# Layer 0 of a hybrid decoder: 111 two-input elementwise instructions issued on VectorE instead of GpSimd

## The chip, the core and the metric

The program runs on one core of one Trainium2 chip. A core has five engines that run side by side, each through its own queue in order: PE (TensorE, matrix products), DVE (VectorE), ACT (ScalarE), POOL (GpSimd) and SP (which here only issues DMAs). PE writes its products to PSUM; DVE, ACT and POOL work on tiles in SBUF, and DVE and ACT also read PSUM. The metric is device microseconds of one execution. Of the kernel before, three runs took 1946.46, 1949.92 and 1953.49 us; the median, 1949.92 us, is the time to compare with.

## The reference

One inference step of a trunk of two layers, 1024 wide, over a prompt of 1024 rows and 8 samples of 4 rows. All is float32. Layer 0 is cut down here to what the change touches; layer 1 (RWKV-7) is not touched.

```
xn = rmsnorm(h, norm_w[0])
u, z_a, q, f, i, z_b = split(xn @ even_w_in)              # 24 blocks of 128 columns
# S5: 32 groups of 16 channels, 64 complex states each
bu = einsum(u, bb);  h_t = ab * h_{t-1} + bu_t            # complex, as a scan
y  = Re(einsum(h, c)) + d * u
y  = gelu(y);  out_a = y * sigmoid(y @ glu_w + glu_b) * silu(z_a)
# HGRN2: 4 heads, a 128x128 state each
log_f = log_sigmoid(f);  k = sigmoid(-f);  q = silu(q)
S_t = diag(f_t) S_{t-1} + k_t v_t^T;  o_t = S_t^T q_t     # in chunks
out_b = o * rsqrt(mean(o*o) + eps) * hgrn_norm_w * silu(z_b)
h = h + concat(out_a, out_b) @ even_w_out
# layer 1: h = h + rwkv7(rmsnorm(h, norm_w[1]));  y = rmsnorm(h, final_norm_w)
```

## The kernel before

The 1056 rows of tokens lie along the free axis, in two halves of 512 and 544 columns (`HALF`; the second holds the samples). A feature tile is 128 partitions by 512 or 544 columns.

A dense product (`dense2`, line 805) is done in three passes: weights and inputs are each split into a high part (ACT copies it rounded, line 70) and a low part (the rest, by a subtraction, line 72), and PE sums high·high, high·low and low·high. `split` does this; with `lo_pool` the subtraction goes to POOL, otherwise to DVE. Weights come by DMA in pieces of 128x512, are split on ACT and DVE, and two buffers of each part stand ready (`wh`, `wl`).

Layer 0 first normalizes the inputs (`normed`: a product on DVE, line 153, then a split, whose subtraction goes to POOL for every second of the 8 feature tiles), for the second half, the first half, and the second half again when it is reloaded. Then three generators run interleaved in `layer0`: `dense` (`proj_in`, the 20 blocks per half that aren't u), `s5s` (8 calls of `s5_part`, four channel groups each) and `heads` (8 calls of `hgrn_head`: four heads for each half). After `proj_in` follow `glu` and `proj_out` of the first half, with `norm1` for layer 1, whose sum of squares is added up over the 8 tiles (line 843); then the same for the second half beside the start of layer 1.

`s5_part` makes tables (two products, line 410, and their sum, line 412), rotations (lines 444, 445 and 446), brings them onto the scan's inputs (lines 460 to 465), scans (line 467) and rotates back (lines 470 to 477). `hgrn_head` takes the gates through a running sum (lines 570 to 573, 599, 600), makes keys and queries for sub-chunks of 32 rows (lines 611 and 614), and lets PE transpose and multiply them. POOL did one of each pair of products in S5, and five instructions of each head (six in the second half, with line 680).

All instructions go through a scheduler: the code is emitted as the generators yield, and the scheduler, by a model of the engines' costs, sets the order of each engine's queue for the whole program. An edit that moves work from one engine to another can therefore shift the order of instructions anywhere, in layer 1 too, with the same instructions in it.

Lines 64 and 66 are copies out of PSUM on ACT and DVE (`evac`); line 404 transposes S5's C tables on PE through one of three PSUM buffers, which a copy has to clear (`cst`, `csw`); lines 626 to 691 are HGRN2's matmuls, 417 to 493 S5's.

Of the kernel before, what the change touches and what calls it, by code (L numbers as in the profile page):

```python
# [14 lines left out]
ALU = mybir.AluOpType  # L15
# [4 lines left out]
NB, NS = 8, 4  # L20
# [16 lines left out]
class Builder:  # L37
# [111 lines left out]
    def normed(self, hf, k, x):  # L149
        n = HALF[hf][1]  # L150
        with self.tc.high_priority():
            y = self.evt("xn")
            self.nc.vector.scalar_tensor_tensor(out=y[:, :n], in0=x[:, :n], scalar=self.nw0[:, k:k + 1],
                                                in1=self.rbc[hf][:, :n], op0=ALU.mult, op1=ALU.mult)
            h, l = self.pair(n)
            self.split(h[:, :n], l[:, :n], y[:, :n], lo_pool=k % 2 == 1)
        return h, l
# [225 lines left out]
    def s5_part(self, sp, m, e):  # L383

        nc, I = self.nc, self.I
        V, G = nc.vector, nc.gpsimd
# [21 lines left out]
        for out, n, pa, pb, sa, sb in ((X, 8, self.xr, self.xi, bst, bsw), (Gt, 9, self.gr, self.gi, cst, csw)):  # L408
            for w, o, p, x in ((V, t1, pa, sa), (G, t2, pb, sb)):
                w.tensor_tensor(out=o[:, :, :n], in0=p[:, gs].unsqueeze(3).broadcast_to([128, 4, n, 16]),  # L410
                                in1=x[:].unsqueeze(2).broadcast_to([128, 4, n, 16]), op=ALU.mult)
            V.tensor_tensor(out=out, in0=t1[:, :, :n], in1=t2[:, :, :n], op=ALU.add)
# [30 lines left out]
        for out, (p, q), (r, s), op in ((cosn, (ir, jr), (ii, ji), ALU.subtract), (sinn, (ii, jr), (ir, ji), ALU.add)):  # L443
            V.tensor_tensor(out=v4(a1), in0=B(p, 0), in1=B(q, 1), op=ALU.mult)
            G.tensor_tensor(out=v4(a2), in0=B(r, 0), in1=B(s, 1), op=ALU.mult)
            V.tensor_tensor(out=out, in0=a1, in1=a2, op=op)
# [17 lines left out]
        f2 = lambda t: t[:].rearrange("p g c -> p (g c)")  # L464
        G.tensor_tensor(out=r1, in0=r1, in1=r2, op=ALU.add)
        Ht = T("Ht", 4, 128)
        V.tensor_tensor_scan(out=f2(Ht), data0=f2(dec), data1=f2(r1), initial=0.0, op0=ALU.mult, op1=ALU.add)

        m1, m2, ms = T("r1", 4, 128), T("r2", 4, 128), T("tb", 4, 128)
        G.tensor_tensor(out=m2, in0=Ht, in1=sinn, op=ALU.mult)  # L470
        V.tensor_tensor(out=m1, in0=Ht, in1=cosn, op=ALU.mult)
# [79 lines left out]
    def hgrn_head(self, sp, hf, h):  # L551
# [20 lines left out]
        V.tensor_tensor_scan(out=b, data0=self.rs[:, :n], data1=lf, initial=0.0, op0=ALU.mult, op1=ALU.add)  # L572
        G.tensor_tensor(out=f, in0=lf, in1=f, op=ALU.subtract)

# [24 lines left out]
        V.tensor_tensor(out=v33(b), in0=v33(b), in1=rr.unsqueeze(2).broadcast_to([128, nr, 32]), op=ALU.subtract)  # L599
        G.tensor_tensor(out=f, in0=f, in1=b, op=ALU.subtract)  # L600
        A.activation(b, b, AF.Exp)
# [7 lines left out]
        for i in (1, 2, 3):  # L609
            kr[i] = T(f"hk{i}", 4, i + 1, 32)  # L610
            (G if i == 3 else V).tensor_tensor(out=kr[i], in0=v4(kl)[:, :, 0:i + 1], in1=offs[i].unsqueeze(3).broadcast_to([128, 4, i + 1, 32]),
                            op=ALU.mult)
        qi = T("hqi", 4, 4, 32)
        G.tensor_tensor(out=qi, in0=v4(q), in1=wq.unsqueeze(3).broadcast_to([128, 4, 4, 32]), op=ALU.mult)

# [53 lines left out]
        if hf:  # L669
            self.dma(O["p_hgrn"][0, 0, h], self.SH[h])  # L670
            ps = PS(32)
            nc.tensor.matmul(ps, vt[:32, 4], self.atts[:32], start=True, stop=False)
            for s in range(NB):
                cs = slice(512 + NS * s, 512 + NS * s + NS)
                nc.tensor.matmul(ps[:, NS * s:NS * s + NS], S0[:, s], q[:, cs], start=False, stop=s == NB - 1)
            self.evac(o[:, 512:544], ps, 32)
            vm = T("hvm", NB, 128)
            V.tensor_tensor(out=vm[:32], in0=vt[:32, 4].unsqueeze(1).broadcast_to([32, NB, 128]),
                            in1=self.bm[:32].unsqueeze(2).broadcast_to([32, NB, 128]), op=ALU.mult)
            G.tensor_tensor(out=S0, in0=S0, in1=pS.unsqueeze(2).broadcast_to([128, NB, 128]), op=ALU.mult)  # L680
            for c in range(2):
                ps = PS(4, 128)
                nc.tensor.matmul(ps, kt[:32, 4], vm[:32, 4 * c:4 * c + 4], start=True, stop=True)
                V.tensor_tensor(out=S0[:, 4 * c:4 * c + 4], in0=S0[:, 4 * c:4 * c + 4], in1=ps, op=ALU.add)
            self.dma(O["s_hgrn"][0, :, h].rearrange("b k v -> k b v"), S0)
# [8 lines left out]
        V.scalar_tensor_tensor(out=o, in0=o, scalar=self.hw, in1=rst, op0=ALU.mult, op1=ALU.mult)  # L694
        G.tensor_tensor(out=o, in0=o, in1=z, op=ALU.mult)
        self.dma(self.cat_d[h][:, c0:c0 + n], o)
# [124 lines left out]
    def norm1(self, hf, temp):  # L821
# [13 lines left out]
        for k, x in enumerate(self.xn):  # L835
# [4 lines left out]
            if k == 0:  # L840
                V.tensor_copy(acc[:, :n], sq[:, :n])
            else:
                G.tensor_tensor(out=acc[:, :n], in0=acc[:, :n], in1=sq[:, :n], op=ALU.add)
        for p0, q in cuts:
# [1164 lines left out]
```

## Time and profile before

| | |
|---|---|
| median of three runs | 1949.92 us (1946.46 to 1953.49) |
| the profiled execution | 1946.68 us, of which the span 1945.0 us |
| PE busy | 1736.1 us, 89% |
| DVE busy | 1256.1 us, 65% |
| ACT busy | 979.8 us, 50% |
| POOL busy | 507.5 us, 26% |
| granted TensorE clock, mean | 0.903 |

The profile is that of one execution. Busy is time in which an instruction of the engine runs, and an engine that is held up inside an instruction counts as busy. PE's matmuls overlap, so its busy time is more than what it would need. The granted clock is a share of full speed (2.4 GHz); PE runs at either that or 1.2 GHz, and a mean between tells how much of a stretch went at each. Layer 0 takes about the first 645 us, then the two layers overlap to about 770 us.

### The profile page before, as it was taken

The numbers are of one execution on the slowest core, as the hardware profiler recorded it, in microseconds if no ns is written. First come the engines' busy times: TensorE is split into PE (matmuls) and PEld (weight loads), VectorE is DVE, ScalarE is ACT, GpSimd is POOL, SyncE is SP. The second block draws the span as 40 slices with busy tenths as digits, with TensorE's granted clock in tenths as the row PEclk, the third lists the DMA queues.
The fourth block names the chain that finished last, engine by engine and source line by source line (L and its number), as shares of the span: only waits on it lengthen the run. The fifth ranks groups of instructions, "written<-read, shape, count | busy, mean of one in ns | idle before, by whom it ended". The sixth has DMA issues, their size and how long they took to land. (4 is left out here: it accounts for less than half of the span.)

```text
span 1945.0 us, 39798 instructions
## 1 busy us (share of the span) xinstructions
PE 1736.1 (89%) x15060; PEld 1437.8 (74%) x15060; DVE 1256.1 (65%) x2700; ACT 979.8 (50%) x1887; POOL 507.5 (26%) x567
## 2 busy tenths in 40 slices
PE   6989889889979689998579999999899999999977
PEld 5767768788868577576447787888788888778776
DVE  5887778655554953689585852478979454655543
ACT  6345656354553434753345756565547434534464
POOL 2413535323221500001042410133322112331231
PEclk9989989887889899898779997999799899998799
DMA  9545444433544446699928424469795666544453
GB/s 242 150 128 153 112 116 134 121 112 107 154 148 152 128 150 199 199 243 263 247 66 219 140 88 129 130 168 276 191 235 160 164 160 166 151 130 128 121 151 112
DMA packets 555013, 308.40 MB, mean 159 GB/s; under 512 B 284884, under 2 KB 489044, under 8 KB 554821
## 3 DMA queue, kind: packets, MB, share of 16 engines
q1 hardware_dynamic: 554820, 305.86, 57.3%
q8 instruction: 119, 1.95, 0.4%
q14 instruction: 74, 0.60, 0.1%
HBM read 199.76 MB, written 104.81 MB: 157 GB/s over the span
## 5 line engine op out<-in xcount | busy, mean ns | idle before, releaser
L805 PE MATMUL dps<-xh,wh 128*128 128x272 f32 (+3 forms) x1696 | 589.5, 353 | 59.4 <-ACT wh L70 25.0
L805 PE MATMUL dps<-xl,wh 128*128 128x272 f32 (+3 forms) x1696 | 585.3, 347 | 7.8 <-DVE xl L72 6.1
L805 PE MATMUL dps<-xh,wl 128*128 128x272 f32 (+3 forms) x1696 | 581.9, 345 | 5.1 <-DVE wl L72 4.9
L805 PEld LDWEIGHTS dps<-xh,wh 128*128 128x128 f32 x1696 | 335.2, 200 | 110.6 <-ACT wh L70 29.9
L805 PEld LDWEIGHTS dps<-xh,wl 128*128 128x128 f32 x1696 | 338.6, 200 | 48.6 <-DVE wl L72 11.2
L805 PEld LDWEIGHTS dps<-xl,wh 128*128 128x128 f32 x1696 | 338.6, 200 | 47.7 <-DVE xl L72 8.2
L70 ACT ACTIVATE wh<-ws 128x512 fp32r<-128x512 f32 (+1 forms) x336 | 198.8, 620 | 331.8 <-PE dps L805 181.7
L72 DVE TENSOR_TENSOR wl<-ws,wh 128x512 fp32r<-128x512 f32 (+1 forms) x321 | 238.2, 756 | 139.3 <-ACT wh L70 125.5
L1514 PE MATMUL m<-ZR,BK 64*128 64x128 f32 x512 | 68.3, 311 | 10.4 <-DMA ZR<-zr 10.4
L1514 PEld LDWEIGHTS m<-ZR,BK 64*128 64x128 f32 x512 | 56.9, 206 | 19.6 <-DMA ZR<-zr 10.5
L70 ACT ACTIVATE xh<-mm 128x256 fp32r<-128x256 f32 (+1 forms) x112 | 52.9, 483 | 34.0 <-DVE mm L944 15.0
L805 PE MATMUL dps<-gh,wh 128*128 128x272 f32 (+1 forms) x176 | 56.3, 321 | 11.3 <-ACT wh L70 4.3
L72 POOL TENSOR_TENSOR xl<-mm,xh 128x256 fp32r<-128x256 f32 (+1 forms) x40 | 33.1, 828 | 111.6 <-ACT xh L70 89.0
L805 PE MATMUL dps<-gh,wl 128*128 128x272 f32 (+1 forms) x176 | 55.4, 316 | 7.3 <-DVE wl L72 7.3
L805 PE MATMUL dps<-gl,wh 128*128 128x272 f32 (+1 forms) x176 | 55.8, 317 | 5.6 <-DVE gl L72 5.6
L1411 DVE TENSOR_TENSOR sT<-sX,sN 128x31 f32<-128x31 f32 (+15 forms) x124 | 50.3, 405 | 5.2 <-DMA sN<-nd 2.8
L1417 DVE TENSOR_TENSOR sX<-sX,sT 128x31 f32<-128x31 f32 (+15 forms) x124 | 50.8, 410 | 2.3
L72 POOL TENSOR_TENSOR e<-ek,e 128x512 fp32r<-128x512 f32 (+1 forms) x16 | 22.0, 1376 | 114.5 <-ACT e L70 87.9
L72 DVE TENSOR_TENSOR xl<-mm,xh 128x512 fp32r<-128x512 f32 (+2 forms) x72 | 42.6, 599 | 12.7 <-PE t L1104 7.3
L64 ACT ACTIVATE ev<-dps 128x272 f32<-128x272 f32 (+1 forms) x65 | 29.4, 452 | 41.9 <-PE dps L805 36.4
L66 DVE COPY ev<-dps 128x272 f32<-128x272 f32 (+1 forms) x43 | 22.4, 523 | 42.9 <-PE dps L805 36.3
L805 PEld LDWEIGHTS dps<-gh,wh 128*128 128x128 f32 x176 | 36.0, 205 | 16.3 <-ACT ev L723 4.8
(651 smaller groups left out, 3676.4 us busy)
## 6 DMA issues: line engine op xcount, KB each, us to landing
ws<-in_rw_w_rkvz SPq DMA_DIRECT2D x128, 256.0 KB
ws<-in_even_w_in SPq DMA_DIRECT2D x96, 256.0 KB
ws<-in_rw_w_o SPq DMA_DIRECT2D x48, 256.0 KB
ws<-in_even_w_out SPq DMA_DIRECT2D x32, 256.0 KB
BK<-bk SPq DMA_DIRECT2D x32, 256.0 KB
ZR<-zr SPq DMA_DIRECT2D x32, 256.0 KB
pr<-ev SPq DMA_DIRECT2D x20, 272.0 KB
pr<-ev SPq DMA_DIRECT2D x20, 256.0 KB
```

Source lines behind the costliest of these rows:

```text
L64: return self.nc.scalar.activation(out, in_, AF.Copy)
L66: return self.nc.vector.tensor_copy(out, in_)
L70: self.nc.scalar.activation(hi, x, AF.Copy)
L72: e.tensor_tensor(out=lo, in0=x, in1=hi.bitcast(F32), op=ALU.subtract)
L805: mm = lambda c0, n, i, u, k, v: self.nc.tensor.matmul(ps[c0], u[:, k, :], v[:, c0:c0 + n], start=i == 0, stop=i == len(terms) - 1)
L1411: E.tensor_tensor(out=w, in0=X[:, s0:s0 + m, j:j + 1].broadcast_to([128, m, n]), in1=N[:, j, j + 1:32].unsqueeze(1).broadcast_to([128, m, ...
L1417: E.tensor_tensor(out=X[:, s0:s0 + m, j + 1:32], in0=X[:, s0:s0 + m, j + 1:32], in1=w, op=ALU.subtract)
L1514: nc.tensor.matmul(f2(pm[h][:, q]), f2(BK[hr, q]), f2(ZR[hr, q]), start=True, stop=True)
```

## The change

Eleven places of layer 0 issue their two-input instruction on DVE (`V`) where it stood on POOL (`G`). In numbers of instructions: 16 of line 410 and 16 of 445, 8 each of 465, 470, 573, 600, 611 (the key of sub-chunk 3), 614 and 695, 4 of 680, the 7 sums of line 843 for the first half, and 12 subtractions of `normed`. That is 111; POOL's queue is 111 rows shorter, and DVE's longer by as many. The operands, sizes and results are the same.

```diff
@@ normed
-            self.split(h[:, :n], l[:, :n], y[:, :n], lo_pool=k % 2 == 1)
+            self.split(h[:, :n], l[:, :n], y[:, :n])
@@ s5_part: tables, rotations, the scan's input, the rotation back
-            for w, o, p, x in ((V, t1, pa, sa), (G, t2, pb, sb)):
+            for w, o, p, x in ((V, t1, pa, sa), (V, t2, pb, sb)):
-            G.tensor_tensor(out=v4(a2), in0=B(r, 0), in1=B(s, 1), op=ALU.mult)
+            V.tensor_tensor(out=v4(a2), in0=B(r, 0), in1=B(s, 1), op=ALU.mult)
-        G.tensor_tensor(out=r1, in0=r1, in1=r2, op=ALU.add)
+        V.tensor_tensor(out=r1, in0=r1, in1=r2, op=ALU.add)
-        G.tensor_tensor(out=m2, in0=Ht, in1=sinn, op=ALU.mult)
+        V.tensor_tensor(out=m2, in0=Ht, in1=sinn, op=ALU.mult)
@@ hgrn_head: gates, keys, queries, the samples' state, the output's gate
-        G.tensor_tensor(out=f, in0=lf, in1=f, op=ALU.subtract)
+        V.tensor_tensor(out=f, in0=lf, in1=f, op=ALU.subtract)
-        G.tensor_tensor(out=f, in0=f, in1=b, op=ALU.subtract)
+        V.tensor_tensor(out=f, in0=f, in1=b, op=ALU.subtract)
-            (G if i == 3 else V).tensor_tensor(out=kr[i], in0=v4(kl)[:, :, 0:i + 1], in1=offs[i].unsqueeze(3).broadcast_to([128, 4, i + 1, 32]),
+            V.tensor_tensor(out=kr[i], in0=v4(kl)[:, :, 0:i + 1], in1=offs[i].unsqueeze(3).broadcast_to([128, 4, i + 1, 32]),
-        G.tensor_tensor(out=qi, in0=v4(q), in1=wq.unsqueeze(3).broadcast_to([128, 4, 4, 32]), op=ALU.mult)
+        V.tensor_tensor(out=qi, in0=v4(q), in1=wq.unsqueeze(3).broadcast_to([128, 4, 4, 32]), op=ALU.mult)
-            G.tensor_tensor(out=S0, in0=S0, in1=pS.unsqueeze(2).broadcast_to([128, NB, 128]), op=ALU.mult)
+            V.tensor_tensor(out=S0, in0=S0, in1=pS.unsqueeze(2).broadcast_to([128, NB, 128]), op=ALU.mult)
-        G.tensor_tensor(out=o, in0=o, in1=z, op=ALU.mult)
+        V.tensor_tensor(out=o, in0=o, in1=z, op=ALU.mult)
@@ norm1
-                G.tensor_tensor(out=acc[:, :n], in0=acc[:, :n], in1=sq[:, :n], op=ALU.add)
+                (G if hf else V).tensor_tensor(out=acc[:, :n], in0=acc[:, :n], in1=sq[:, :n], op=ALU.add)
```

The scheduler's order moves with it. DVE's queue of the kernel before, at one S5 part's rotations (`cosn` and `sinn` from the products `ta` and `tb`; `tb` is POOL's):

```order
L444 TENSOR_TENSOR ta<-ir,jr 128x512
L72 TENSOR_TENSOR wl<-ws,wh 128x512
L446 TENSOR_TENSOR cosn<-ta,tb 128x512
L72 TENSOR_TENSOR wl<-ws,wh 128x512
L444 TENSOR_TENSOR ta<-ii,jr 128x512
L446 TENSOR_TENSOR sinn<-ta,tb 128x512
L410 TENSOR_TENSOR ta<-xr,bst 128x4x128
```

DVE's queue of the changed kernel, at a part's rotations beside the gates of a head (`hl`, `hf`, `hb`, `hex`) and the second normalization of the reloaded tiles (`xn`, `xl`):

```order
L573 TENSOR_TENSOR hf<-hl,hf 128x512
L72 TENSOR_TENSOR xl<-xn,xh 128x544
L432 TENSOR_TENSOR KK<-KK,dd 16x4x16
L153 SCALAR_TENSOR_TENSOR xn<-x,nw_208,rbc_235 128x544
L446 TENSOR_TENSOR cosn<-ta,tb 128x512
L577 COPY hrr<-hb 128x16
L589 TENSOR_TENSOR hex<-hb 128x4
L72 TENSOR_TENSOR xl<-xn,xh 128x544
L594 MEMSET hrr 128x1
L430 TENSOR_TENSOR dd<-ident,dT 16x64
L444 TENSOR_TENSOR ta<-ii,jr 128x512
L445 TENSOR_TENSOR tb<-ir,ji 128x512
```

Lines 445 and 573 now stand in DVE's own queue between its other work, and every subtraction of `xl` does.

PE's queue of the kernel before where `proj_in` ends (272 columns) and `glu` of the first half begins (`gh`, `gl`, 512 columns); the last head is done by then:

```order
L805 MATMUL dps<-xh,wh 128x272
L805 MATMUL dps<-xl,wh 128x272
L805 MATMUL dps<-xh,wl 128x272
L805 MATMUL dps<-gh,wh 128x512
L805 MATMUL dps<-gl,wh 128x512
L805 MATMUL dps<-gh,wl 128x512
```

The same place in PE's queue of the changed kernel:

```order
L805 MATMUL dps<-xl,wh 128x272
L805 MATMUL dps<-xh,wl 128x272
L805 MATMUL dps<-gh,wh 128x512
L805 MATMUL dps<-gl,wh 128x512
L805 MATMUL dps<-gh,wl 128x512
L626 MATMUL xh<-ident,hk_5403 128x128 x4
L630 MATMUL xh<-ident,hke 32x128
L640 MATMUL xh<-hq,hf 32x32
```

The transposes and products of the last head come after the end of `proj_in` instead of before it. S5's and HGRN2's matmuls between stand later among the dense ones too, by some 50 to 120 places on average.

DVE's queue of the changed kernel during `proj_out` of the first half, where `norm1` adds up its squares (line 843) and `glu` of the second half fetches its inputs (`y`, lines 711 and 713):

```order
L757 TENSOR_TENSOR h_5998<-h_5998,dps 128x512
L72 TENSOR_TENSOR wl<-ws,wh 128x512 x2
L841 COPY n<-n 128x512
L843 TENSOR_TENSOR n<-n 128x512
L757 TENSOR_TENSOR h_6037<-h_6037,dps 128x512
L72 TENSOR_TENSOR wl<-ws,wh 128x512
L711 COPY y<-yl 128x8x64
```

Line 843 was not in this queue before, and the copies of line 711 stood ahead of the first line 757.

## Rows read from the trace of the kernel before

**Rows 1.** The page's head: span, and busy time of each engine.

```profile
span 1945.0 us, 39798 instructions
PE 1736.1 (89%) x15060; PEld 1437.8 (74%) x15060; DVE 1256.1 (65%) x2700; ACT 979.8 (50%) x1887; POOL 507.5 (26%) x567
```

**Rows 2.** Busy time by stretch: us, then PE, PEld, DVE, ACT, POOL, clock, DMA, GB/s.

```profile
200.00:350.00 150.00, 126.95 (x747) 107.26 (x746) 119.11 (x209) 89.08 (x133) 70.86 (x75) 0.91 0.44 122
350.00:560.00 210.00, 193.84 (x1251) 173.56 (x1250) 113.78 (x224) 98.68 (x155) 59.80 (x48) 0.85 0.41 121
1000.00:1945.00 945.00, 883.10 (x10082) 741.51 (x10080) 578.67 (x1282) 496.73 (x1083) 237.60 (x266) 0.92 0.59 157
```

**Rows 3.** What PE waited for from 75 to 645 us: us, times, longest.

```profile
PE xs L404 <- DVE cst L66: 8.1, 1, 8.1
PE dps L805 <- ACT ev L181: 7.3, 7, 1.9
PE dps L805 <- ACT wh L70: 6.6, 1, 6.6
PE xh L626 <- POOL hk L611: 5.1, 3, 3.1
PE xs L458 <- DVE KK L66: 4.7, 2, 4.1
PE dps L805 <- DVE xl L72: 2.3, 1, 2.3
```

**Rows 4.** Line views, one tile Ht on both engines, and two others: ns min/median/max.

```profile
L470 POOL TENSOR_TENSOR r<-Ht,sinn x8: 1266/1616/1802, 190.4 to 477.6; 128x512 f32<-128x512 f32 x8
L471 DVE TENSOR_TENSOR r<-Ht,cosn x8: 672/691/1415, 190.4 to 480.5; 128x512 f32<-128x512 f32 x8
L72 DVE TENSOR_TENSOR xl<-xn,xh x16: 679/712/1855, 25.4 to 1076.8; 128x544 fp32r<-128x544 f32 x8, 128x512 fp32r<-128x512 f32 x8
L678 DVE TENSOR_TENSOR hvm<-hvt,bm x4: 1206/2010/2334, 363.6 to 525.6; 32x1024 f32<-32x1024 f32 x4
```

**Rows 5.** Timeline of DVE and POOL at one rotation: start, us, instruction.

```profile
265.10 0.77 DVE L444 TENSOR_TENSOR ta<-ir,jr 128x512 f32<-128x512 f32 x1
...
265.29 1.50 POOL L445 TENSOR_TENSOR tb<-ii,ji 128x512 f32<-128x512 f32 x1
...
268.02 1.45 POOL L445 TENSOR_TENSOR tb<-ir,ji 128x512 f32<-128x512 f32 x1 [1.23 <-DVE cosn L446]
...
268.47 1.55 DVE L444 TENSOR_TENSOR ta<-ii,jr 128x512 f32<-128x512 f32 x1
```

**Rows 6.** Timeline of DVE: the first and last of 67 stretched rows to 720 us.

```profile
26.22 1.68 DVE L153 SCALAR_TENSOR_TENSOR xn<-x,nw,rbc 128x544 f32<-128x544 f32 x1
...
519.85 1.48 DVE L711 COPY y<-yl 128x512 f32<-128x512 f32 x1
```

**Rows 7.** Waits: DVE's for POOL, 0 to 645 us; last, POOL's at line 680.

```profile
DVE hS L684 <- POOL hS L680: 5.4, 3, 1.8
...
DVE X L412 <- POOL tb L410: 4.6, 2, 3.6
DVE G L412 <- POOL tb L410: 3.8, 3, 1.3
...
POOL hS L680 <- PE xh L675: 27.2, 3, 17.1
```

**Rows 8.** Timeline before PE's longest wait, that for line 404.

```profile
285.42 1.27 POOL L470 TENSOR_TENSOR r<-Ht,sinn 128x512 f32<-128x512 f32 x1 [2.05 <-DVE Ht L467]
285.49 1.28 DVE L590 COPY hex<-hrr 128x4 f32<-128x4 f32 x1
...
290.50 0.36 PE L404 MATMUL xs<-ident,cl 64*128 64x64 f32 x1 [8.13 <-DVE cst L66]
```

**Rows 9.** Granted clock after two of PE's waits: stretches as in rows 2.

```profile
306.00:313.00 7.00, 6.94 (x43) 5.68 (x42) 7.00 (x11) 2.44 (x5) 5.95 (x10) 0.76 0.76 258
...
409.00:413.00 4.00, 4.00 (x21) 4.00 (x22) 4.00 (x19) 1.94 (x3) 0.01 (x1) 0.57 0.46 151
```

## The prediction

> **What bounds the kernel now.** I began with the page's head [rows 1]: PE is busy for 89% of the span, DVE for 65%, POOL for 26%. POOL is no bound by its share; the question is who waits for it, and where. So the second view is busy time by stretch [rows 2], over the part in which most of the moved instructions lie, 79 of the 111. PE has little room there: 127 of 150 us from 200 to 350, 194 of 210 from 350 to 560. Yet it isn't at its best: its clock is granted at 0.91 and 0.85 of full speed. DVE is the second busiest, and from 200 to 350 us nearly full, 119 of 150 us. The third view is what PE waited for [rows 3]. The dense products wait for little; most of the waits are those of S5's and HGRN2's small matmuls, for a DVE copy (8.1 and 4.7 us), for POOL's key `hk` (5.1) and for a split (2.3). These four make 20 us and all end on DVE or POOL. Two more, 7.3 and 6.6 us, end on ACT. A wait costs more than itself: after those near 305 and 409 us the clock stood at 0.76 and 0.57 for 7 and 4 us [rows 9].
>
> So the bound is PE, with short waits in which DVE's queue, in order, has not come to the instruction that PE needs. The last view is why DVE is late: one rotation [rows 5]. The first product on line 444 began 0.19 us before POOL's on line 445 and took 0.77 us. The other, of the same size, began 0.45 us after POOL's next, took 1.55 us, and ended 0.55 us after POOL did. DVE did not work through POOL's instruction; it was held inside its own until POOL ended. Line by line this recurs: line 471 has a median of 691 ns and a longest of 1415, line 72's `xl` 712 and 1855 [rows 4].
>
> **The change part by part.**
>
> *What DVE gets.* 111 instructions. At full width each costs what DVE's twin does undisturbed: 0.69 us at 512 columns (line 471), 0.71 at 544, and 1.21 at 1024 (line 678's shortest) [rows 4]. 107 x 0.70 + 4 x 1.21 = 80 us, of which 30 (43 instructions) lie from 200 to 350 us.
>
> *What DVE loses in stretching.* For every DVE row of the timeline up to 720 us I took its length less the shortest of its line and size. It adds to 89 us. 67 rows, the first and last in [rows 6], are longer by over 0.1 us and lie beside POOL instructions that the change removes more than beside those it leaves: 60 us together, 28 of them from 200 to 350 us. Another 18 us lie beside instructions that stay on POOL and remain. The bounds: 60 if POOL was the cause of each, 0 if POOL only stood beside it. I take 60, since in [rows 5] the end of DVE's instruction follows POOL's end.
>
> *What DVE loses in waiting for POOL.* The sums of lines 684 and 412 waited for POOL's half of a pair, 5.4 + 4.6 + 3.8 = 14 us [rows 7], 1 of them from 200 to 350 us. Now both halves come in one queue.
>
> Together: +80 - 60 - 14 = +6 us over all, and +30 - 28 - 1 = +1 from 200 to 350 us. DVE's queue advances as it did, although 80 us of work came to it.
>
> *What the chains get.* The two-input product took POOL 1.6 us and takes DVE 0.69 [rows 4], so the chains of S5 and HGRN2 shorten by 0.9 us at each of several steps. In PE's longest wait [rows 8], the copy `cst` came 8.1 us late; in these 8 us DVE was held three times by POOL (line 590, a copy of 4 columns, took 1.28 us beside line 470), some 3 us in all by the same reckoning, but now lines 465, 470 and 600 would take 2 us in that queue. This wait shrinks by only 1 us if the order stays, and goes where the order gives it room.
>
> *What the new order gives.* The scheduler puts the small matmuls later among the dense ones, and the last head after `proj_in`'s end. PE's work is the same, and the dense products don't need these results, so PE asks later for what DVE makes at the same pace as before. A hundred places at 150/747 = 0.20 or 210/1251 = 0.17 us a matmul [rows 2] are 17 to 20 us of room, more than any of the four waits. Of the 20 us I therefore take 14 as gone. Bounds: all 20 go, or none, because new ones open elsewhere; I stay nearer to the upper end, as the room exceeds each wait. The clock adds to that: 7 us at 0.76 and 4 us at 0.57 lost 7 x 0.24 + 4 x 0.43 = 3.4 us [rows 9]; I take 3. The 14 us that end on ACT stay: no work leaves ACT.
>
> *What may cost.* The added instructions wait for nearly nothing new: their inputs come from DVE's line before. Two do. Line 680 waits for PE, as it overwrites what line 675 reads; POOL waited there up to 17 us [rows 7]. On DVE the next splits and copies would be queued behind it, and PE waits for those. But in three of the four heads it now stands behind a copy of line 675's result, for which DVE waits anyway. I take 0 to 7 us: nothing in three cases, and in the fourth (27.2 - 17.1)/2 = 5 us, the mean of the two shorter of POOL's waits, and some 2 for what it delays. Line 843 waits for ACT's square, with the next block's `wl` and sum behind it (line 757). It waits for ACT to finish one instruction of a block of 24 matmuls; I take 0, at most 0.7 us x 7 = 5. The last head's DVE work, some 17 instructions' worth at 0.7 us or 12 us, moves into `glu` and `proj_out`, and line 711 after it; there DVE has room, so 0.
>
> *Layer 1.* Its instructions are the same, in an order that differs from 1000 us on. PE is busy for 883 of 945 us there [rows 2], so 62 us are open to chance; a tenth of it, 6 us either way, is my estimate for another order.
>
> Sum: 14 + 3 = 17 us gained, less some 5 for small new waits, half of the 12 that lines 680 and 843 could cost at most: 12 us. The profiled execution took 1946.7 us, 1945.0 of it the span; it comes to 1935. The median of the runs is 3.2 us above that execution, so I forecast 1938 us.
>
> The Trainium skill, "Perfetto Trace Analysis", section "Optimizing Scalar/DVE Operations", speaks against the direction of the move: a saturated DVE may be relieved by giving work to ScalarE or even GpSimd, though it adds that GpSimd shares a port with DVE and that moving between those two might not help. By its first half DVE from 200 to 350 us would go from 119 to 149 of 150 us and the change would lose; by its second half the 28 us come back. The first half is the rival below.
>
> The Trainium skill, "SBUF — State Buffer", section "Who interferes with whom", says that a DVE instruction with two SBUF inputs and a GpSimd instruction that reads SBUF exclude one another for their whole length. The trace agrees, with 1.55 us for 0.77 in [rows 5]. By it the moved instructions can be held in turn by what stays on POOL; that would give back part of the 60 us, an estimate of a quarter, as a quarter of POOL's time in layer 0 stays.
>
> **The rivals.**
>
> *DVE becomes the bound (slower).* If the stretched time isn't POOL's doing, or returns beside what stays there, DVE's queue from 200 to 350 us holds up to 149 us in 150. It then can't take the waits for ACT that it has there, and each `wl` and `xl` comes late for the dense products. Half of the 30 us would land on PE: 1950 + 15 = 1965. It decides from the point where less than about 15 of the 28 us come back. For it: 79% busy already. Against it: [rows 5], and line 590 in [rows 8].
>
> *Nothing to be seen.* The four waits go, and as many open elsewhere: the copies and splits that PE waits for still stand in one DVE queue, now with 111 more rows in front. 1946 to 1950; I put it at 1948. For it: the wait for line 404 shrinks by only 1 us in its own place. Against it: the later asking.
>
> *The order of layer 1 costs more than layer 0 gains.* The whole program was ordered anew. With 6 us more there, and 5 of layer 0's gain left, 1951; a bad place behind a weight's split could make it 1958.
>
> *More than forecast.* All 20 us go, and ACT's 6.6 us with its clock phase: 1950 - 20 - 7 - 5 = 1918.
>
> **How the numbers follow.** Chances: the forecast, between 1928 and 1944, 0.52; more than that 0.10; nothing to be seen 0.20; DVE the bound 0.10; layer 1's order 0.08. The range must leave out no more than two in ten: from 1920, near the best case, to 1958, which holds layer 1's order and leaves out most of DVE as the bound. A measurement of this kernel can tell about 0.3%, 6 us, from no change: faster is below 1944. That is the first two cases, 0.62; the same 0.22 (the third, and a little of the last); slower 0.16.
>
> **What would show it.** Right: DVE's busy time up to 645 us within some 20 us of before, with line 444 near 0.69 us on average, line 72's `wl` too, and no wait of DVE for POOL on lines 412 and 684; PE's waits for `cst`, `hk` and `KK` together below 10 us; the end of `proj_out` of the first half earlier by about 12 us. Wrong: DVE from 200 to 350 us at over 140 of 150 us, with PE waiting for `wl` or `xl`; or layer 0 ending earlier and the span from 1000 us on longer by as much. If line 444 stays near 1 us without POOL beside it, the step on stretching fails, and with it the forecast.

## The result, and the profile of the changed kernel

The changed kernel takes 1926.08 us (median of 4 runs, 1921.69 to 1933.61), beside 1951.70 us (4 runs) for the kernel before: a ratio of 0.9872, 95% interval 0.9829 to 0.9916. The forecast was 1938 us, between 1920 and 1958. The profiled execution took 1924.02 us.

The page's head, which answers to [rows 1], and then what DVE waited for from 75 to 590 us on lines 684, 843 and 680 (us, times, longest; compare [rows 7]):

```profile
span 1922.3 us, 39712 instructions
...
PE 1741.3 (91%) x15060; PEld 1442.8 (75%) x15060; DVE 1270.5 (66%) x2811; ACT 977.3 (51%) x1885; POOL 352.2 (18%) x456
```

```profile
DVE hS L684 <- PE xh L683: 3.0, 3, 1.9
...
DVE n L843 <- ACT n L837: 0.9, 2, 0.8
...
DVE hS L680 <- PE xh L675: 0.2, 1, 0.2
```

POOL lost 155 us of work; DVE took over 111 instructions and is busy for only 14 us more. No wait of DVE for POOL is left up to 590 us. The two new waits on which the prediction had spent up to 12 us, on lines 680 and 843, are 0.2 and 0.9 us.

The span divides well where the first half is normalized for layer 1 (line 848, DVE's RECIPROCAL, at 634.1 us before and 590.1 us after): layer 0 ends there for the first half, and what is left of it for the second half runs beside the start of layer 1. Busy time by stretch, columns as in [rows 2], of the kernel before and then of the changed one:

```profile
0.00:634.10 634.10, 554.87 (x3108) 469.53 (x3108) 418.13 (x934) 321.82 (x530) 213.70 (x225) 0.90 0.49 140
634.10:1945.00 1310.90, 1181.27 (x11953) 968.24 (x11953) 837.94 (x1767) 657.94 (x1358) 293.78 (x342) 0.90 0.62 167
```

```profile
0.00:590.10 590.10, 536.19 (x3107) 455.81 (x3107) 428.25 (x1044) 323.57 (x531) 50.62 (x114) 0.94 0.54 151
590.10:1922.30 1332.20, 1205.06 (x11953) 986.96 (x11953) 842.21 (x1767) 653.72 (x1355) 301.53 (x342) 0.89 0.61 165
200.00:350.00 150.00, 133.01 (x833) 116.54 (x832) 121.59 (x258) 94.97 (x141) 8.65 (x29) 0.93 0.47 130
```

So layer 0 gained 44.0 us and the rest gave back 21.3. In layer 0, PE ran the same matmuls (3108 and 3107 records) in 19 us less busy time, at a clock of 0.94 instead of 0.90, and its idle time fell from 79 to 54 us. In the rest, PE's idle time barely moved (130 and 127 us); its busy time rose by 24 us, for the same 11953 matmuls. The loss there goes with the clock, whose mean is 0.904 before and 0.891 now: some 19 us of work at full speed over 1332 us, by an estimate from these two.

What PE waited for from 75 us to the end of layer 0, the changed kernel; these are the eight largest, and they answer to [rows 3]:

```profile
PE dps L805 <- ACT ev L181: 14.5, 6, 4.0
PE dps L805 <- DVE xl L72: 5.9, 4, 2.3
PE dps L805 <- ACT ev L64: 2.1, 2, 1.7
PE dps L805 <- DVE wl L72: 1.9, 2, 1.6
PE dps L805 <- ACT xh L70: 1.6, 1, 1.6
PE xh L626 <- DMA hi<-pr: 1.2, 2, 1.0
PE xs L417 <- ACT csw L64: 1.2, 1, 1.2
PE dps L805 <- DVE ev L66: 1.0, 2, 0.9
```

Of the waits for `cst`, `KK` and `hk` in [rows 3], 17.9 us, 1.3 are left (`cst` 0.8, `hk` 0.5); that for `xl` grew from 2.3 to 5.9. On ACT, the wait for `wh` fell from 6.6 to 0.9 and that for `ev` of line 181 rose from 7.3 to 14.5. Summed over the whole list, waits that end on DVE or POOL fell from 33.3 to 10.7 us, those that end on ACT only from 24.4 to 21.9. One line of DVE, minimum, median and maximum in ns as in [rows 4]:

```profile
L471 DVE TENSOR_TENSOR r<-Ht,cosn x8: 672/684/685, 188.4 to 438.2; 128x512 f32<-128x512 f32 x8
```

Its longest was 1415 ns; none of the eight is held now. Reckoned as in the prediction (each DVE row's length less the shortest of its line and size, here over all kernels, up to the end of layer 0), the stretching fell from 94 to 35 us.

### The profile page after: what moved, and what is told of

It is laid out like the page before. It is cut to its first block, busy times and chain, and to the rows that moved or that the text cites. A ratio compares the mean times of both kernels' runs of the same rounds, so it can differ in the third digit from the quotient of the medians.

```text
span 1922.3 us, 39712 instructions
## 1 busy us (share of the span) xinstructions
PE 1741.3 (91%) x15060; PEld 1442.8 (75%) x15060; DVE 1270.5 (66%) x2811; ACT 977.3 (51%) x1885; POOL 352.2 (18%) x456
## 5 line engine op out<-in xcount | busy, mean ns | idle before, releaser
L805 PEld LDWEIGHTS dps<-xh,wl 128*128 128x128 f32 x1696 | 339.0, 201 | 48.4 <-DVE wl L72 15.7
L72 DVE TENSOR_TENSOR wl<-ws,wh 128x512 fp32r<-128x512 f32 (+1 forms) x321 | 230.8, 732 | 136.1 <-ACT wh L70 128.2
L70 ACT ACTIVATE xh<-mm 128x256 fp32r<-128x256 f32 (+1 forms) x112 | 52.4, 481 | 27.7 <-DVE mm L929 10.7
L1411 DVE TENSOR_TENSOR sT<-sX,sN 128x31 f32<-128x31 f32 (+15 forms) x124 | 52.0, 419 | 11.2 <-DMA sN<-nd 9.1
L1541 PE MATMUL m<-L,MZ 64*64 64x64 f32 x512 | 39.3, 247 | 7.8 <-DVE L L66 5.7
L66 DVE COPY ev<-dps 128x272 f32<-128x272 f32 (+1 forms) x43 | 22.5, 523 | 35.7 <-PE dps L805 30.8
```

The source lines that it names most:

```text
L66: return self.nc.vector.tensor_copy(out, in_)
L70: self.nc.scalar.activation(hi, x, AF.Copy)
L72: e.tensor_tensor(out=lo, in0=x, in1=hi.bitcast(F32), op=ALU.subtract)
L805: mm = lambda c0, n, i, u, k, v: self.nc.tensor.matmul(ps[c0], u[:, k, :], v[:, c0:c0 + n], start=i == 0, stop=i == len(terms) - 1)
L1411: E.tensor_tensor(out=w, in0=X[:, s0:s0 + m, j:j + 1].broadcast_to([128, m, n]), in1=N[:, j, j + 1:32].unsqueeze(1).broadcast_to([128, m, ...
L1541: nc.tensor.matmul(pm[hr, q], MZ[kr, q, h], L[kr, q, h], start=True, stop=True)
```

## The experiments

Two questions were open: whether POOL's reading is what held DVE inside its instructions, with the gain divided among the parts as the held time was; and where the 21 us of the rest come from. For the second there were two theories. One is the order: the whole program is scheduled anew, and layer 1's instructions, which the change doesn't touch, come in another order. The other is that a layer 1 that follows a faster layer 0 runs slower, in whatever order.

A measure for the order: for each small instruction of PE from the second half's normalization for layer 1 (line 846) on, how many dense matmuls (line 805) stand before it, and by how many that differs from another kernel, on average. It looks at PE's queue alone; those of DVE and ACT move with it. The kernel before and the changed one differ by 19.0. The expectations go by the last stage, from the second half's line 848 to the end: 950 us before, 975 in the changed kernel. All kernels in one table; "layer 0" and "rest" are parted at line 848 as above, "DVE, POOL" is what PE waited for DVE and POOL from 75 us to the end of layer 0, "stretch" is as above, "-" where it wasn't reckoned. Times are those of the profiled execution in us, the ratio is that of the medians to the kernel before.

| kernel | layer 0 | DVE, POOL | stretch | rest | order: from before / after | ratio, 95% interval |
|---|---|---|---|---|---|---|
| before | 634.1 | 33.3 | 94 | 1310.9 | 0 / 19.0 | 1 |
| changed | 590.1 | 10.7 | 35 | 1332.2 | 19.0 / 0 | 0.9872 (0.9829 to 0.9916) |
| e1, S5 alone | 632.3 | 25.1 | 74 | 1331.7 | 17.5 / 4.3 | 1.0130 (1.0085 to 1.0174) |
| e2, HGRN2 alone | 602.2 | 22.5 | 66 | 1337.3 | 19.0 / 0.2 | 0.9977 (0.9949 to 1.0006) |
| e3, splits alone | 616.1 | 24.2 | 83 | 1335.2 | 16.6 / 5.3 | 1.0047 (1.0016 to 1.0078) |
| e4, products added on POOL | 675.4 | 64.0 | 92 | 1317.2 | 7.5 / 12.8 | 1.0293 (1.0240 to 1.0346) |
| e5, fills added on POOL | 649.6 | 41.2 | 37 | 1321.7 | 16.6 / 18.8 | 1.0073 (1.0038 to 1.0107) |
| e6, line 680 back | 588.3 | 8.3 | - | 1332.5 | 8.1 / 12.2 | 0.9829 (0.9780 to 0.9879) |
| e7, all but S5 | 601.6 | 14.0 | 59 | 1321.4 | 5.7 / 15.7 | 0.9872 (0.9830 to 0.9914) |
| e8, all but HGRN2 | 618.4 | 24.8 | 64 | 1332.9 | 9.1 / 13.4 | 0.9997 (0.9969 to 1.0025) |
| e9, order of before | 581.6 | 8.7 | 39 | 1304.7 | 0 / 19.0 | 0.9793 (0.9743 to 0.9843) |
| e10, order of changed | 579.6 | 10.4 | - | 1328.7 | 17.5 / 4.3 | 0.9859 (0.9807 to 0.9911) |
| e11, third key back | 608.7 | 18.8 | - | 1315.9 | 3.5 / 20.4 | 0.9847 (0.9794 to 0.9901) |
| e12, lines 843 and 721 | 589.2 | 11.2 | - | 1303.5 | 3.5 / 20.4 | 0.9732 (0.9702 to 0.9762) |

The stages of a row come from one execution, up to 13 us from its kernel's median: e9's is 13 us below, e11's 12 and e5's 9 above. Four kernels with nearly the same order in layer 0 (changed, e6, e10, e12) lie at 580 to 590 us there, so that a difference of 10 us in these columns tells little.

**The parts alone.** e1 makes the hunks of lines 409 to 470 of the diff alone, e2 those of lines 573 to 695, e3 that of line 156 with its sum on line 843 left as it was. One line of each:

```diff
-            G.tensor_tensor(out=v4(a2), in0=B(r, 0), in1=B(s, 1), op=ALU.mult)
+            V.tensor_tensor(out=v4(a2), in0=B(r, 0), in1=B(s, 1), op=ALU.mult)
...
-        G.tensor_tensor(out=f, in0=lf, in1=f, op=ALU.subtract)
+        V.tensor_tensor(out=f, in0=lf, in1=f, op=ALU.subtract)
...
-            self.split(h[:, :n], l[:, :n], y[:, :n], lo_pool=k % 2 == 1)
+            self.split(h[:, :n], l[:, :n], y[:, :n])
```

> Only S5's 48 instructions move (lines 410, 445, 465, 470). Layer 0 is timed by the start of the reciprocal of line 848: 634.1 us before, 590.1 after. The held-up theory (DVE is held inside its instruction while POOL reads) takes the gain from the stretched time beside each moved group: S5's lines made about 23 of 60 us of it, so about 44 x 23/60 = 17 us of the gain, 617 us. The order theory (what counts is that the scheduler asks for the small matmuls later) leaves it open. Layer 1 from its own reciprocal (994.6 before, 947.0 after) to the end took 950 us before and 975 after; the order of PE's queue in layer 1 is here nearly that of after (small matmuls 4 places off, 17 from before): if that order costs the 25 us, layer 1 takes 965 to 975; if a faster layer 0 costs them, some 960.

> Only HGRN2's 44 instructions move (lines 573, 600, 611, 614, 680, 695). The held-up theory: HGRN2's lines made about 25 of the 60 us of stretched time, so about 18 us of the 44, line 848 at 616 us. Layer 1's order on PE is that of after (0.2 places off): if order makes the 25 us, layer 1 takes 973 to 977 us and the whole is slower than before less 18: about 1952; if the speed of layer 0 makes them, layer 1 takes 960.

> Only the 12 subtractions of normed move. Layer 0: 12 of 60 us of stretched time are theirs, of which little lies beside PE's waits: line 848 at 625 to 634 us. Layer 1's order is near that of after (5 places off, 17 from before) behind a layer 0 like that of before. Order theory: layer 1 takes 965 to 975 us, and the whole is slower than before, about 1965. Speed-of-layer-0 theory: layer 1 takes 950 to 955, the whole 1945.

Layer 0 gained 2, 32 and 18 us, where 17, 18 and at most 9 were expected: 52 together, against 44 for all at once. So the gain doesn't follow the stretch that each part takes away (20, 28 and 11 us); S5 alone removes 20 us of it and gains almost nothing. PE's waits for DVE and POOL fell by 8 us, but its clock in layer 0 stood at 0.89, and of the waits those for the dense products' operands now lead. What PE waited for in e1, up to 650 us:

```profile
PE dps L805 <- DVE wl L72: 11.8, 4, 6.3
PE dps L805 <- ACT ev L64: 7.8, 5, 3.3
PE dps L805 <- ACT wh L70: 5.5, 2, 3.0
```

All three kernels have a slow rest, 1332 to 1337 us; their last stages took 978, 984 and 973 us, as slow as the order wanted or slower. In e1 it follows a layer 0 that is as slow as before. That speaks against the theory of the faster layer 0, and for the order, which in all three lies within 5.3 places of that of the changed kernel.

**POOL's reading, put back.** To the changed kernel 104 additions on POOL are made, at the places of the moved instructions of layer 0; no result depends on them. Each addition is a copy of one column of what DVE made there and, in e4, a product that reads two full tiles; in e5, three fills, which read nothing. POOL is busy for 248 and 244 us in layer 0.

```diff
+    G.tensor_copy(self.scr[:, 0:1], x)
+    G.tensor_tensor(out=self.scr[:, :n], in0=self.gc[:, :n], in1=self.gc[:, :n], op=ALU.mult)
```

```diff
+    G.tensor_copy(self.scr[:, 0:1], x)
+    for c in (544, 544, 272):
+        G.memset(self.scr[:, :c], 0.0)
```

> The changed kernel, and on POOL beside each of 104 of the moved instructions an instruction that reads two tiles nobody else uses and writes one nobody reads (1.3 us each, some 135 us of POOL's time come back; no result depends on them). Held-up theory: DVE's rows are stretched again, by 40 to 60 us in all, line 444 has instructions of 1.4 us and over, and most of the gain of layer 0 goes: line 848 at 615 to 635 us. Chain theory (what counts is 0.69 us in place of 1.6 us in each chain): line 848 stays at 590 to 600, line 444 at 0.69.

> The changed kernel with 104 additions on POOL at the places of the previous run, but here each addition is a copy of one column and three fills of a scratch tile, which read nothing, instead of a product that reads two tiles. No result depends on them. If POOL's reading of SBUF holds DVE up, DVE's instructions are not lengthened (line 444 below 0.72 us on average, as in the changed kernel) and layer 0 ends near 590 to 615 us, the total below 1945 us. If what cost the previous run its time was POOL's queue with more in it, and the copies and waits that came with it, layer 0 ends near 675 us again and the total is about 2000 us.

Line 471 of e4, then of e5, columns as above:

```profile
L471 DVE TENSOR_TENSOR r<-Ht,cosn x8: 677/680/1524, 182.0 to 564.0; 128x512 f32<-128x512 f32 x8
```

```profile
L471 DVE TENSOR_TENSOR r<-Ht,cosn x8: 680/683/693, 176.2 to 541.0; 128x512 f32<-128x512 f32 x8
```

With reading products the stretch of DVE is back at 92 us, with fills it stays at 37, as without any additions (35). POOL's work of the same length that, but for the copied columns, reads nothing doesn't hold DVE. The Trainium skill, "SBUF — State Buffer", section "Who interferes with whom", says that a DVE instruction with two SBUF inputs contends with a GpSimd instruction that reads SBUF and not with one that only writes it; by 92 and 37 us, the traces agree.

The times are another matter. e4 is slower than e5 by 26 us in layer 0 and by 2.2% in the ratios: that goes with 55 us more of stretch. But the levels were missed: e4's layer 0 is at 675 us, not at 615 to 635, and e5's neither at 590 to 615 us, as that theory wanted, nor at 675, as the rival did. The additions cost 60 us without any stretch to speak of, and e4 is slower than even the kernel before, which has as much stretch. Part of it can be seen: waits of PE, and one of DVE, in e5:

```profile
PE xs L426 <- DVE G L412: 25.8, 4, 10.4
PE xs L492 <- DMA TP<-KK: 10.6, 3, 5.4
```

```profile
DVE tb L410 <- POOL scr L1984: 5.0, 1, 5.0
```

The small copies of POOL wait for DVE, all of POOL's S5 work is queued behind them, and DVE waits in turn before it may overwrite what they read. Layer 0's order changed as well: by the measure above, here over the 1101 small instructions of PE ahead of line 846, both kernels have them some 310 dense matmuls from their places in the changed kernel, but only 1.6 from each other's. So their times in layer 0 can be compared with each other, and neither with that of the changed kernel. How much of the 60 us is the queue and how much the order wasn't settled.

**The order, first round.** e6 is the changed kernel with line 680 put back on POOL, e7 the kernel before with all but S5's hunks, e8 with all but HGRN2's.

```diff
-            V.tensor_tensor(out=S0, in0=S0, in1=pS.unsqueeze(2).broadcast_to([128, NB, 128]), op=ALU.mult)
+            G.tensor_tensor(out=S0, in0=S0, in1=pS.unsqueeze(2).broadcast_to([128, NB, 128]), op=ALU.mult)
```

> The changed kernel with line 680 alone put back on POOL (4 instructions). Layer 0 should end as in the changed kernel, 590 us, 600 at most. What this shift does is to give layer 1 another order: its small work on PE lies some 8 dense matmuls from its place in the kernel before and 12 from that in the changed kernel, on average (the two kernels themselves are 19 apart). If the order of layer 1 costs the changed kernel its 25 us there, the last stage, from the second block's first normalization on, takes 950 to 965 us instead of 975, and the total is 1900 to 1915 us. If a layer 1 that starts sooner is slower whatever its order, the last stage takes 975 us or more and the total is 1925 us.

> HGRN2's instructions, the splits and the sum of line 843 move to DVE, S5's stay on POOL. Layer 1's small work stands 6 dense matmuls from its place in the kernel before, on average, and 16 from that in the changed kernel, so by the theory of the order the last stage takes 950 to 960 us; by the theory that a fast layer 0 makes layer 1 slow, 970 or more. Layer 0: if the two parts alone add up, 634 - 32 - 18 = 584 us; if S5's part is worth what the held-up instructions say, about 15 us more than in the changed kernel, 605. Total by order and adding up: 1895 to 1905 us; by the other theories 1925 to 1945.

> S5's instructions, the splits and the sum of line 843 move to DVE, HGRN2's stay on POOL. If the parts add up, layer 0 ends at 634 - 2 - 18 = 614 us; if S5's part only pays where the others are gone too, at 605 or below. Layer 1's small work stands 9 dense matmuls from its place in the kernel before and 13 from the changed one, so by the theory of the order the last stage takes 952 to 968 us; by the other, that it goes by layer 0's pace, 965 or more. Total 1920 to 1935.

The last stage took 971, 959 and 971 us. Only e7, the nearest to the order of before, came out as the order wanted; e6 and e8, with places between the two orders, missed by 6 and 3 us. The totals missed as well, e6's by 2 us, those of e7 and e8 by 19 and 16. For the order this round is inconclusive. For layer 0 it tells that S5's part is worth 11 us on top of the others (601.6 to 590.1), HGRN2's 28 (618.4 to 590.1). In e7 line 444 is held as before, 1547 ns at most; in the changed kernel it takes 693.

e7 also tells of a rival in layer 0, that PE only asks later. In the changed kernel the small instructions of PE in layer 0 stand 67 dense matmuls from their places in the kernel before, nearly all of them later; in e7 they lie 16 from there, 4 later on the whole, and layer 0 is 32 us shorter all the same. So most of the gain doesn't need the later order; what the order adds was in no run tested alone.

**The order, second round.** Small shifts in layer 0 make the scheduler choose one order or the other for all of layer 1. e9 puts lines 680 and 695 back on POOL and moves line 721 (`za`, 8 instructions of `glu`) to DVE; layer 1 on PE is then in the order of before, matmul for matmul. e10 leaves out the shift of line 695 and has nearly the order of the changed kernel. Their lines, the second only in e9:

```diff
-            V.tensor_tensor(out=S0, in0=S0, in1=pS.unsqueeze(2).broadcast_to([128, NB, 128]), op=ALU.mult)
+            G.tensor_tensor(out=S0, in0=S0, in1=pS.unsqueeze(2).broadcast_to([128, NB, 128]), op=ALU.mult)
...
-        V.tensor_tensor(out=o, in0=o, in1=z, op=ALU.mult)
+        G.tensor_tensor(out=o, in0=o, in1=z, op=ALU.mult)
...
-            G.tensor_tensor(out=za[:, :n], in0=za[:, :n], in1=ys[m][:, :n], op=ALU.mult)
+            V.tensor_tensor(out=za[:, :n], in0=za[:, :n], in1=ys[m][:, :n], op=ALU.mult)
```

> The changed kernel with lines 680 and 695 (12 instructions) put back on POOL and line 721 of glu (8 instructions) moved to DVE: small shifts in layer 0, which leave layer 1's PE work in exactly the order of the kernel before, matmul for matmul. The theory of the order: the last stage, from the second block's first normalization on, takes 950 to 960 us as in the kernel before, with PE busy about 888 us in it at a clock near 0.92 and without the gap some 270 us in, after which the changed kernel's clock stands at 0.50; layer 0 ends near 590 to 600 us, the total is 1898 to 1912 us, and the kernel beats both. The theory that a layer 1 which follows a faster layer 0 is slower, in whatever order: 970 us or more, total 1920 to 1930.

> The control to the run before it: the same without the shift of line 695, so line 680 on POOL and line 721 on DVE. Layer 0 should be the same within some 5 us (590 to 600). Layer 1's small work on PE now lies 3 dense matmuls from its place in the changed kernel, on average, and 18 from that in the kernel before. The theory of the order: the last stage takes 970 to 985 us, PE busy 905 or more in it, with the gap some 270 us in and a clock near 0.50 behind it; total 1920 to 1932 us. If the order doesn't decide, the two runs are equal within 6 us.

Layer 0 is the same in both, 581.6 and 579.6 us, some 10 us less than expected; what follows isn't. Their two stretches, e9 and then e10:

```profile
0.00:581.60 581.60, 531.79 (x3108) 452.46 (x3108) 425.68 (x1039) 324.30 (x531) 61.47 (x120) 0.94 0.54 153
581.60:1886.30 1304.70, 1169.99 (x11953) 958.95 (x11953) 833.49 (x1769) 658.12 (x1358) 298.56 (x340) 0.91 0.62 168
```

```profile
0.00:579.60 579.60, 531.11 (x3108) 454.98 (x3108) 426.88 (x1047) 317.38 (x527) 46.94 (x112) 0.94 0.54 154
579.60:1908.30 1328.70, 1208.15 (x11953) 990.43 (x11953) 842.36 (x1769) 654.78 (x1355) 296.75 (x340) 0.89 0.60 165
```

PE is busy for 38 us less in e9, and idle for 14 more: 24 us net. The last stage took 941 us, less than the 950 to 960 expected, and 975, as expected. The medians are 1901 us, as expected, and 1915, 5 us less than expected. They differ by 14 us, and the intervals of the ratios overlap, so that two more kernels were run. e11 puts the third key of line 611 back on POOL. e12 exchanges two lines: 843 back on POOL, 721 to DVE.

```diff
-            V.tensor_tensor(out=kr[i], in0=v4(kl)[:, :, 0:i + 1], in1=offs[i].unsqueeze(3).broadcast_to([128, 4, i + 1, 32]),
+            (G if i == 3 else V).tensor_tensor(out=kr[i], in0=v4(kl)[:, :, 0:i + 1], in1=offs[i].unsqueeze(3).broadcast_to([128, 4, i + 1, 32]),
```

```diff
-                (G if hf else V).tensor_tensor(out=acc[:, :n], in0=acc[:, :n], in1=sq[:, :n], op=ALU.add)
+                G.tensor_tensor(out=acc[:, :n], in0=acc[:, :n], in1=sq[:, :n], op=ALU.add)
...
-            G.tensor_tensor(out=za[:, :n], in0=za[:, :n], in1=ys[m][:, :n], op=ALU.mult)
+            V.tensor_tensor(out=za[:, :n], in0=za[:, :n], in1=ys[m][:, :n], op=ALU.mult)
```

> The changed kernel with only the third key product of line 611 (8 instructions) put back on POOL, as in the kernel before. Layer 1's small work lies 3.5 dense matmuls from its place in the kernel before, 22 from that in the changed one. The theory of the order: last stage 950 to 962 us, no gap 270 us in; layer 0 ends near 592 to 600 us, as 8 of the moved instructions can hold DVE again; total 1900 to 1915 us. Otherwise 1922 to 1932 us.

> The changed kernel with line 843 (7 instructions) back on POOL and line 721 (8 instructions) on DVE instead; S5's and HGRN2's instructions and the splits stay on DVE. A second way to the order of before: layer 1's small work on PE lies 3.5 dense matmuls from its place in the kernel before, on average, and 22 from that in the changed kernel. The theory of the order: layer 0 ends near 580 to 592 us, what follows takes 1303 to 1318 us (the kernel before 1311, the changed one 1332), with the clock at full speed where the changed one has its gap; total 1895 to 1910 us. If the order is not what costs, 1328 us or more follow and the total is 1912 to 1925 us.

e11's rest came as expected (1315.9 us, its last stage 952), its layer 0 didn't (609 us). e12 settles it: layer 0 as in the changed kernel, to 0.9 us, and the rest shorter by 28.7 us. Its last stage, in which none of the shifted lines runs, took 940 us against 975. Its two stretches:

```profile
0.00:589.20 589.20, 534.10 (x3107) 454.81 (x3107) 426.57 (x1044) 322.19 (x530) 47.89 (x115) 0.94 0.53 151
589.20:1892.70 1303.50, 1176.76 (x11953) 965.70 (x11953) 839.25 (x1769) 657.41 (x1358) 297.76 (x340) 0.91 0.62 168
```

Its median is 1893.01 us (6 runs, 1889.27 to 1898.24; 2 us below what was expected), 0.9732 (0.9702 to 0.9762) of the kernel before. It beats both kernels; its interval lies clear of that of the changed one.

Over all kernels, the four whose order lies within 3.5 places of that of before have a rest of 1304 to 1316 us, the five within 5.3 of that of the changed kernel 1329 to 1337, and the five others lie at 1317 to 1333. The pace of layer 0 doesn't sort them: it is 634 and 582 to 609 us in the first group, 632 and 580 to 616 in the second.

**Where the order costs.** Some 270 us into the last stage. Busy time by stretch of the changed kernel there, then of e12 at the same distance (its last stage begins at 952.3 us, that of the changed kernel at 947.0):

```profile
1217.00:1227.00 10.00, 5.82 (x88) 4.43 (x90) 8.90 (x17) 6.63 (x18) 3.95 (x6) 0.72 0.28 50
1227.00:1237.00 10.00, 10.00 (x76) 7.70 (x76) 7.36 (x19) 7.86 (x20) 2.07 (x4) 0.50 0.28 55
1237.00:1247.00 10.00, 10.00 (x64) 9.51 (x64) 6.52 (x13) 1.24 (x2) 4.27 (x6) 0.76 0.65 179
1247.00:1257.00 10.00, 9.76 (x90) 8.60 (x89) 4.36 (x9) 5.38 (x9) 2.60 (x3) 1.00 0.91 250
1257.00:1267.00 10.00, 10.00 (x76) 7.03 (x76) 4.16 (x6) 3.39 (x7) 3.19 (x3) 0.59 0.63 181
1267.00:1277.00 10.00, 10.00 (x74) 9.00 (x70) 4.13 (x8) 0.54 (x2) 0.77 (x1) 0.72 0.69 199
```

```profile
1222.00:1232.00 10.00, 9.46 (x192) 7.67 (x191) 9.83 (x27) 7.95 (x24) 2.02 (x5) 1.00 0.48 121
1232.00:1242.00 10.00, 9.42 (x128) 7.52 (x128) 8.84 (x23) 6.56 (x17) 5.09 (x7) 1.00 0.49 93
1242.00:1252.00 10.00, 10.00 (x107) 9.27 (x103) 9.09 (x20) 5.33 (x14) 2.96 (x3) 1.00 0.76 200
```

In the changed kernel PE is idle for 4.2 of the first 10 us, and in the following 50 us its clock stands at 0.50, 0.76, 1.00, 0.59 and 0.72. At these clocks the 56 us of busy time hold 40 us of work at full speed: 16 us lost, and 4 idle. In e12 the clock stays at 1.00. What PE waits for in the gap, from its timeline in the changed kernel:

```profile
1220.61 0.52 PE L805 MATMUL dps<-xh,wh 128*128 128x272 f32 x2 [1.58 <-ACT xh L70]
...
1226.22 0.82 PE L805 MATMUL dps<-xh,wh 128*128 128x272 f32 x2 [2.48 <-ACT xh L70]
```

Dense products ask for a split of a mixed input (`mm`, lines 936 to 944) that ACT and DVE make only then, with the keys and sums of lines 1322 to 1348 between. Two waits, 4.1 us together, and PE's small products around them. e12 has no wait of over 0.4 us from 1200 to 1250 us.

The other kernels lose in the same place. The stretch from the 721st to the 1081st of the last stage's 2520 dense matmuls, in the changed kernel, in e10, in the kernel before and in e12:

```profile
1220.60:1340.90 120.30, 112.95 (x1348) 98.31 (x1349) 86.39 (x175) 56.41 (x130) 40.76 (x47) 0.83 0.75 197
```

```profile
1211.30:1329.30 118.00, 109.95 (x1328) 97.39 (x1329) 84.20 (x170) 54.23 (x125) 36.77 (x47) 0.84 0.76 200
```

```profile
1274.60:1362.20 87.60, 83.39 (x1244) 74.62 (x1241) 68.71 (x134) 49.75 (x114) 32.49 (x39) 1.00 0.88 229
```

```profile
1227.50:1318.10 90.60, 86.04 (x1243) 76.98 (x1241) 71.46 (x138) 51.99 (x120) 35.81 (x41) 0.96 0.87 228
```

All five kernels near the order of the changed one take 117 to 120 us there, at a clock of 0.83 to 0.85; the four near that of before take 88 to 91, at 0.96 to 1.00. The longer stretch holds some 85 to 105 small matmuls more, so the work is not quite the same; at the end of the stage the two of the changed order shown here are 25 to 35 us behind the other two.

## Why the prediction was right, and where its terms were off

*What bounds the kernel, and the mechanism: right.* DVE was held by what POOL read, PE waited for DVE, and most of both went. The bounds of the stretching step were 0 and 60 of 89 us, and 60 was taken: 59 went, by the table above. The lengths of DVE's rows in layer 0 add up to 475 us before and 496 after, and these 21 us more are the 80 that came less the 59 that went; its busy time grew by only 10, as neighbouring rows overlap in the trace. DVE from 200 to 350 us is busy for 121.6 us, against 119.1 in [rows 2], where the rival that makes DVE the bound wanted up to 149. Up to the end of layer 0 it is busy for 428.3 us instead of 418.1. The mark set for it, within some 20 us of before up to 645 us, was missed in its letter, 478 us beside 429, since by then the changed kernel is 44 us further on. e4 and e5, in the same order in layer 0, show by themselves what stretches DVE, and that 55 us of it go with 26 us of layer 0. How the 44 us divide among stretch and order isn't shown, and e1, where 20 us of stretch went for 2 us, says that stretch alone doesn't give the gain. The 1.6 us that the prediction gave for POOL's product is line 470's median; those of lines 410, 445 and 465 are 1.1 to 1.5, so that the chains shorten by less. No term of its sum rested on that. Of the quarter that the prediction, by the rule on the shared port, saw given back to the instructions that stay on POOL, little came: 35 us of stretch remain, where 94 less 60 would be 34.

*DVE's waits for POOL: right*, 14 us to none; three more, on lines 467 and 446, had made 5 us and went too. *The new waits: over-rated*, 12 us at most and 5 taken (half of 12 is 6), where lines 680 and 843 cost 0.2 and 0.9.

*PE's waits: the term of 14 us measured 23.* The prediction counted four waits of [rows 3], 20 us. Between the last two lines shown there the list has larger ones, two of them of dense products for DVE:

```profile
PE dps L805 <- DVE ev L66: 4.2, 3, 3.1
PE dps L805 <- DVE wl L72: 3.1, 2, 2.9
```

The whole list up to 634 us has 33 us that end on DVE or POOL, and two thirds of it went, though `xl`, one of the four, grew. The waits that end on ACT stayed in their sum, as said. The reason given, that PE asks later, isn't what most of the gain rests on: e7 has 32 us of it, and waits of 14.0 us for DVE and POOL, with hardly any of the later order.

*The clock: the term of 3 us measured 19.* This is the step that was most wrong in layer 0. It was priced by the two slow phases after two waits [rows 9]; what moved was the mean clock of all 555 us of PE's busy time, 0.90 to 0.94. The sum for layer 0 was 12 us; measured were 25 us less of PE's idle time, 23 of it waits for DVE and POOL, and 19 less of its busy time, which make the 44. That the clock rose because the waits went is argued from [rows 9] and from e4 and e5 (more waits, clocks of 0.86 and 0.88); no run moved the one without the other.

*Layer 1: the term of 6 us either way measured 21, to the bad side.* The prediction had it as a rival and took a tenth of PE's idle time as its size. The idle time was the wrong view: it didn't change. The order worked on the clock, as the stretch of 117 to 120 us at 0.83 to 0.85 shows, so that all 1181 us of busy time were open to it. The prediction's sign of being wrong, a later part longer by as much as layer 0 is shorter, came half true.

So two errors of opposite sign, 32 us too little for layer 0 and 21 too much for the rest, left 1926 us beside a forecast of 1938. That they nearly cancel, so that the total came within 12 us, is luck. The forecast's case, from 1928 to 1944, was narrowly missed below, and the range held. The rival "more than forecast", 1918 us, came nearest in its total. Its reasons came true in part: ACT's wait for `wh` did go, 6.6 to 0.9 us, but that for `ev` of line 181 grew by 7.2; and it didn't reckon with the 21 us of the rest.

## What to carry to other kernels

When work is moved off POOL, count what POOL's reading held up on DVE, not POOL's busy share: here 80 us of added work made DVE's rows longer by 21 us in sum, as 59 us of stretching went. Price a wait of PE together with the granted clock of its whole stretch: in layer 0 PE's busy time fell by 19 us at a higher clock, beside 25 us of idle time. And if a scheduler orders the whole program, time the stages apart: a stage that the change doesn't touch gave back half of the gain, and a swap of 15 instructions elsewhere brought that back and 7 us more.

## What the runs showed of the hardware

Fills on POOL, 104 times three of them, left line 471 on DVE at 693 ns at most and DVE's stretch at 37 us, as without them (35), while products that read brought 1524 ns and 92 us back. A gap of 4 us in PE's work was followed by 50 us in which the clock fell to 0.50 and, after a stretch at 1.00, to 0.59 again, although PE was idle for only 0.2 us of them; with the same work in another order it stood at 1.00 in that place.
